# A transformer block on one core: a PSUM bank moved from products to scores, and the dilated heads' transposes issued behind the next group's scores

## The chip, the cores and the metric

The kernel runs on one core of a Trainium2 chip. The metric is the device time of one execution in microseconds. Three runs of the kernel before took 2779.58, 2775.93 and 2775.42 us; their median is 2775.93 us. A fourth execution was profiled, and all rows below are from it.

## The reference

One block on a sequence of 2048 tokens of width 1024, float32. A conditioning vector gives scales, shifts and gates for two normalisations. The normalised input goes through one product with a 1024 x 2816 matrix (IN_WIDTH), whose columns feed three mixers; their outputs are put together, multiplied with `w_out`, gated and added to x. A feed-forward part with a causal convolution of width 3 and a final normalisation follow. The mixers, cut:

```
def _spatial_gating(u, v, g_sgu, w_sp, b_sp):          # "a": 4 groups of 64
    u, v = gelu(u), rmsnorm(gelu(v).reshape(..., 4, 64))
    mixed = einsum('gts,bnsgc->bntgc', tril(w_sp), v) + b_sp
    return u * mixed

def _stick_breaking(q, k, v):                          # 6 heads of 64
    z = einsum('bqhd,bkhd->bhqk', q_blk, k) * scale
    log_beta = log_sigmoid(z)
    log_stay = where(before, log_sigmoid(-z), 0.0)
    tail = cumsum(log_stay, axis=3, reverse=True) - log_stay
    weight = where(before, exp(log_beta + tail), 0.0)
    return einsum('bhqk,bkhd->bqhd', weight, v)

def _dilated_window(q, k, v):                          # 6 heads of 64, dilations 1, 1, 4, 4, 16, 16
    idx = q_pos - offsets * dil                        # 129 offsets: every dil-th key back
    z = einsum('bqhd,bqmhd->bqhm', q_blk, k[idx]) * scale
    z = where(idx >= 0, z, -inf)
    p = exp(z - max(z)); denom = sum(p)
    o = einsum('bqhm,bqmhd->bqhd', p, v[idx]) / denom
    return o, max(z) + log(denom)                      # then weighed over the three dilations
```

## The kernel before, in words

The sequence is worked in 2 chunks of 1024 tokens, each in 2 groups of 512. Every product is made of three matmuls: both factors are split into a high and a low part (fp32r), and high x high, high x low and low x high are added in PSUM. Operands that come from PSUM are therefore stored twice: a copy gives the high part, a subtraction on VectorE (DVE) the low part.

The input product is cut into units of weight columns. `unit_t` (matmuls at L100 to L102, tile `gm`, 24 matmuls of 512 columns) makes transposed queries and keys; `unit_v` (L342, tile `gmv`, 48 matmuls of 256 columns) makes values. Each product fills one PSUM bank and is copied out of it in halves by ScalarE (ACT), DVE or both: `stage<-gm` for queries and keys, `vst<-gmv` for values. The weights are loaded by DMA as `wraw` and split into `whi` (mostly on ACT, L70) and `wlo`.

`stick(h, c)` works one stick-breaking head. Per block of 128 queries and 512 keys: scores into a bank (tile `z`, L534 to L537), two sigmoids on ACT (L539, L540, the second writes back into the bank), a scan along the keys on DVE (`excl<-z`, L545), a product on GpSimd (`beta`), transposes into a bank (tile `tr`, L554), high and low copies (`wh`, `wl`), and the matmuls with the values (tile `av`, L565). The bank of the scores is free once the scan has read it.

`dilated(h)` works one head of the dilated mixer in a loop over 8 groups of 256 queries (two blocks of 128). Per group: scores of both blocks in one bank (`zc`, L620 and L621), mask and maximum on DVE (`ec<-zc`, L623, tile `stat`), its negative (`mx`, L625), the exponential with its sum on ACT (L632), transposes into a bank (`trc`, L635), high and low copies (`whc`, `wlc`), and matmuls with the values (`avc`, L658). Two groups share one `avc` bank, which is then folded and stored.

PSUM has 8 banks. From the start to the marker `rel` (0 to some 785 us) one pool, `ps`, serves all of this: 3 banks for products (tag gm), 2 for scores of both mixers (z), 2 for transposes (tr) and 1 for weighted values (av). Behind `rel` a new pool, `ps2`, has 2 for products and 3 for scores. The first group's products (L910) are made in banks given by name, 4 for queries and keys (`("gm", "gm", "gm", "z")`) and 2 for values.

The string `ORDER` says in which order units of the product and heads are traced, with units interleaved between the steps of heads. Within it, a scheduler with a simulated timeline (`TileContext(schedule_with_timeline_sim=True)`) sets the order of the instructions of each engine; `tc.issue_after(x)` adds an edge that keeps what is traced under it behind instruction x. On the chip each engine then works its instructions strictly in that order.

Of the kernel before, what the change touches and what calls it, by code (L numbers as in the profile page):

```python
# [5 lines left out]
F32 = mybir.dt.float32  # L6
# [3 lines left out]
AF = mybir.ActivationFunctionType  # L10
# [5 lines left out]
P = 128  # L16
# [27 lines left out]
class Kernel:  # L44
# [529 lines left out]
    def dilated(self, h):  # L574
        nc = self.nc
        pair, row = h // 2, (h % 2) * 64
        d = DIL[pair]
        u, col = (6 + h) // 4, ((6 + h) % 4) * P
        vd = self.vd[u]

        def vloads(gg):
            def f(v):
                if d == 1:
                    return [(v, vd[gg][:, col:col + P].rearrange("(b p) f -> p b f", p=P))]
                if d == 4:
                    return [(v[:, 4 * r + 2 * cc:4 * r + 2 * cc + 2, :],
                             vd[cc].rearrange("(b p r) f -> r p b f", r=4, p=P)[2 * gg + r, :, :, col:col + P])
                            for r in range(2) for cc in range(2)]
                return [(v[64 * cc:64 * cc + 64],
                         vd[cc].rearrange("(p r) f -> p r f", r=16)[:, 8 * gg:8 * gg + 8, col:col + P])  # L590
                        for cc in range(2)]
            return f

        khat, vhat = [], []
        for gg in range(2):
            khat.append(self.head_keys(self.ck[pair][h % 2, :, :, gg * T:(gg + 1) * T]))
            vhat.append(self.head_values(vloads(gg)))
        stat = self.pa.tile([P, 16, 2], F32, name="stat", tag="stat")
        mx = self.pa.tile([P, 16], F32, name="mx", tag="mx")
        per = 16 // d  # L600
        for g in range(8):
            if g % 2 == 0:
                q1, q2 = self.head_queries(self.cq[pair][h % 2, :, :, g * 256:g * 256 + 512])
            qo = (g % 2) * 256
            z = self.ps.tile([P, 2, 256], F32, name="zc", tag="z")
            e = self.pa.tile([P, 2, 256], F32, name="ec", tag="beta")
            for j in range(2):
                blk = 2 * g + j
                first = blk % per == 0
                qs = slice(qo + j * P, qo + (j + 1) * P)  # L610
                qa, qb = q1[:, qs], q2[:, qs]
                own = khat[blk // 8][:, (blk % 8) * P:(blk % 8 + 1) * P]
                if first:
                    spans = [(slice(P, 2 * P), own)]
                elif blk % 8 == 0:
                    spans = [(slice(0, P), khat[blk // 8 - 1][:, 7 * P:8 * P]), (slice(P, 2 * P), own)]
                else:
                    spans = [(slice(0, 2 * P), khat[blk // 8][:, (blk % 8 - 1) * P:(blk % 8 + 1) * P])]
                for sl, kk in spans:
                    nc.tensor.matmul(z[:, j, sl], qa, kk, start=True, stop=False)  # L620
                    nc.tensor.matmul(z[:, j, sl], qb, kk, start=False, stop=True)  # L621
                ks = slice(P, 2 * P) if first else slice(0, 2 * P)
                nc.vector.tensor_tensor_reduce(e[:, j, ks], z[:, j, ks], self.mask[:, ks], 0.125, -3.0e38,  # L623
                                               ALU.add, ALU.max, stat[:, blk, 0:1])
            nc.vector.tensor_scalar(out=mx[:, 2 * g:2 * g + 2], in0=stat[:, 2 * g:2 * g + 2, 0], scalar1=-1.0,  # L625
                                    scalar2=None, op0=ALU.mult)
            tr = self.ps.tile([P, 4, P], F32, name="trc", tag="tr")
            for j in range(2):
                blk = 2 * g + j
                first = blk % per == 0  # L630
                ks = slice(P, 2 * P) if first else slice(0, 2 * P)
                nc.scalar.activation(e[:, j, ks], e[:, j, ks], AF.Exp, bias=mx[:, blk:blk + 1],  # L632
                                     accum_out=stat[:, blk, 1:2])
                for m in ((1,) if first else (0, 1)):
                    nc.tensor.transpose(tr[:, 2 * j + m, :], e[:, j, m * P:(m + 1) * P], self.ident)  # L635
            wh = self.pa.tile([P, 4, P], F32R, name="whc", tag="wh")
            wl = self.pa.tile([P, 4, P], F32R, name="wlc", tag="wl")
            if (2 * g) % per and (2 * g + 1) % per:
                parts = [slice(0, 4)]
            elif (2 * g) % per == 0 and (2 * g + 1) % per == 0:  # L640
                parts = [slice(1, 4, 2)]
            else:
                parts = [slice(1, 4)]
            for sl in parts:
                self.copy("whi_d", wh[:, sl, :], tr[:, sl, :])
                self.tt("v", wl[:, sl, :], tr[:, sl, :], wh[:, sl, :].bitcast(F32), ALU.subtract)
            if g % 2 == 0:
                av2 = self.ps.tile([P, 512], F32, name="avc", tag="av")
            av = av2[:, qo:qo + 256]
            kb = 2 * g  # L650
            if per == 1:
                sets = [[(kb + j, j, 1, 2 * j + 1)] for j in range(2)]
            else:
                sets = [[(kb, 0, 2, 1), (kb + 1, 1, 1, 3)] + ([(kb - 1, 0, 1, 0)] if kb % per else [])]
            for ops in sets:
                for n, (k, j, m, o) in enumerate(ops):
                    for x, w in enumerate((wh, wl)):
                        nc.tensor.matmul(av[:, j * P:(j + m) * P], vhat[k // 8][:, k % 8, :], w[:, o:o + m, :],  # L658
                                         start=(n == 0 and x == 0), stop=(n == len(ops) - 1 and x == 1))
            if g % 2 == 1:  # L660
                ys = self.pa.tile([64, 512], F32, name="ys", tag="ys")
                self.fold(ys, av2, 512)
                self.load(self.yc[pair][row:row + 64, (g // 2) * 512:(g // 2 + 1) * 512], ys)
        sd = self.statd[h]
        if d == 1:
            self.load(sd.rearrange("(b p) s -> p b s", p=P), stat)
        elif d == 4:
            for r in range(4):
                self.load(sd.rearrange("(b p r) s -> r p b s", r=4, p=P)[r], stat[:, 4 * r:4 * r + 4, :])
        else:  # L670
            self.load(sd.rearrange("(p r) s -> p r s", r=16), stat)
# [183 lines left out]
    def run(self):  # L855
# [44 lines left out]
        def qk_cols(p):  # L900
# [6 lines left out]
        near = (self.p1, "whi"), (self.p1, "wlo")  # L907
        places = ((near, near), (near, ((self.pa, "khat"), (self.pa, "khat"))),
                  (((self.pa, "vhat"), (self.pa, "khat")), ((self.pa, "vhat"), (self.pa, "wl"))))
        banks = [self.ps.tile([P, TG], F32, name="gm", tag=tag) for tag in ("gm", "gm", "gm", "z")]  # L910
        vbanks = [self.ps.tile([P, 2, 256], F32, name="gmv", tag=tag) for tag in ("z", "av")]
        for q in range(4):
            self.ada_first(q)
# [133 lines left out]
        for c, order in enumerate(ORDER):  # L1047
            u = units(c, hT[c])
            for token in order.split():
# [38 lines left out]
                elif what == "rope":  # L1088
                    cs = self.rope_tables(c)
                elif what == "ada":  # L1090
                    with tc.issue_after(self.stored.ins):
                        ada[n] = self.ada_rest(n)
                elif what == "dil":
                    finish([f"cqk{n // 2}{c}", f"v{(6 + n) // 4}{c}"])
                    self.dilated(n)
                elif what == "scales":
                    self.dilated_scales()
                elif what == "rel":
                    finish()
                    self.p1.release()  # L1100
                    self.ps.release()
                    self.ps = _Bufs(self.pool("ps2", space=PSUM), {**BUFS, "gm": 2, "z": 3})
                    self.po = _Bufs(self.pool("po"), BUFS)
                elif what == "free":
                    finish()
                    self.pa.release()
                    self.pw = _Bufs(self.pool("pw", side="right"), BUFS)
                    self.pn = _Bufs(self.pool("pn", side="right"), BUFS)
# [43 lines left out]

ENGINES = {"whi0": "a", "wlo0": "v", "lnt0": "a", "hlo0": "v", "lnt": "va", "lnx00": "avv", "lnx01": "aav", "lnx10": "v", "lnx11": "v", "lnx": "va", "hlo": "v", "whi": "a", "wlo": "v", "qkhi": "avv", "qklo": "v", "cqk": "a", "rot1": "v", "rot2": "v", "rot3": "v", "rothi": "aav", "rotlo": "v", "sgu1": "v", "sgu2": "v", "sguhi": "a", "sgulo": "v", "ya": "aaav", "fold": "a", "beta": "p", "whi_s": "a", "whi_d": "avv", "wom": "v", "wohi": "aav", "wolo": "v", "ysc": "v", "yhi": "av", "ylo": "v", "wuhi": "v", "wulo": "pvv", "wdm": "p", "wdhi": "av", "wdlo": "ppv", "upc": "av", "gv": "pppv", "ghi": "ap", "glo": "ppv", "vhi": "av", "vlo": "v", "uc": "v"}

BUFS = {"gm": 3, "z": 2, "tr": 2, "av": 1, "wraw": 2, "whi": 3, "wlo": 3, "s8": 3, "cs": 2, "tmp2": 2, "khat": 3, "vhat": 2, "q": 2, "beta": 4, "excl": 3, "wh": 2, "wl": 2, "fold": 1, "ys": 1, "stat": 2, "mx": 2, "x4": 2, "yraw": 2, "ysc": 4, "yh": 2, "yl": 2, "xo": 3, "wuraw": 4, "wul": 3, "wuh": 3, "wdraw": 2, "fx": 2, "up": 3, "dn": 5, "wdh": 2, "wdl": 2, "upc": 3, "cv": 3, "gh": 4, "gl": 4, "fs": 4, "fry": 2, "frr": 2}

WOUT = 6
EARLY = (0, 1, 5, 6, 7)
# [39 lines left out]
```

## Time and profile before

| | us |
|---|---|
| median of three runs | 2775.93 |
| the profiled execution | 2772.08 |
| its span, first to last instruction | 2770.4 |
| TensorE matmul busy | 2626.6 (95%) |
| VectorE busy | 2109.4 (76%) |
| ScalarE busy | 1025.6 (37%) |
| GpSimd busy | 857.5 (31%) |

The mean granted clock of TensorE was 0.981 of full speed. "Busy" counts the time in which at least one instruction of that engine was executing; matmuls overlap, so that one of 0.39 us can start every 0.23 us. A row of the timeline gives start, duration, engine, line and operands, and in brackets how long the engine stood idle before and what ended it. A name in a row is that of the tile in the code: `z` and `zc` are scores, `tr` and `trc` transposes, `gm` and `gmv` products.

### The profile page before, as it was taken

The page shows a single profiled execution, that of the slowest core. Times are in us where ns is not written, and L with a number is a line of the kernel's source. Part 1 is how long each engine was busy: PE and PEld are TensorE (multiplying, and loading weights), DVE is VectorE, ACT ScalarE, POOL GpSimd, SP SyncE. Part 2 cuts the span into 40 slices and gives each one's busy share as a digit, 9 for nine tenths or more (in the row PEclk, how much of TensorE's full clock was granted, in tenths as well). Part 3 has the DMA queues.
Part 4 walks back from the last instruction along what each step waited for, and adds up shares of the span by engine and source line. Part 5 has one row for each costly group of instructions (what it writes and reads, how often), then busy time and mean ns, then how long its engine had stood idle before and what let it go on. Part 6 is the DMA issues. An engine that isn't in the chain of part 4 may idle for free.

```text
span 2770.4 us, 36801 instructions
## 1 busy us (share of the span) xinstructions
PE 2626.6 (95%) x13430; PEld 2201.3 (79%) x13430; DVE 2109.4 (76%) x3227; ACT 1025.6 (37%) x1918; POOL 857.5 (31%) x878
## 2 busy tenths in 40 slices
PE   6989999899878999999999999999999999999998
PEld 5878998889857777877788888888877888888886
DVE  5487877666689988756877778777888778777877
ACT  5355554444556666534121212111462111121114
POOL 0032101110045444303334443433433433433423
PEclk9999999999999999999999999999999999999999
DMA  7645586789563333286111111111233111111111
GB/s 238 195 131 171 186 266 190 204 211 233 135 186 101 109 111 86 61 275 219 46 46 46 54 51 49 48 52 46 77 103 107 49 47 54 46 46 46 46 38 61
DMA packets 305296, 309.37 MB, mean 112 GB/s; under 512 B 65516, under 2 KB 245596, under 8 KB 305116
## 3 DMA queue, kind: packets, MB, share of 16 engines
q1 hardware_dynamic: 305116, 307.02, 37.6%
q8 instruction: 107, 1.75, 0.3%
q14 instruction: 73, 0.60, 0.1%
HBM read 232.36 MB, written 68.30 MB: 109 GB/s over the span
## 4 chain that ended last, share of the span: by engine, by line
PE 65%; DVE 14%; DMA 10%; ACT 6%; issue 3%; SPq 1%; POOL 0%; DVEq 0%; ACTq 0%; POOLq 0%
PE up L94 11%; PE up L93 11%; PE up L92 11%; PE dn L94 5%; PE dn L92 5%; PE dn L93 5%; DVE excl L545 3%; DMA wraw<-in_w_in_dram 2%; PE gmv L342 2%; DMA wada<-in_w_ada_dram 2%; PE av L565 2%; DVE wl L78 1%; PE gm L100 1%; PE tr L554 1%; PE gm L101 1%
## 5 line engine op out<-in xcount | busy, mean ns | idle before, releaser
L92 PE MATMUL up<-gh,wuh 128*128 128x512 f32 x1408 | 553.4, 393 | 2.1 <-ACT gh L260 2.1
L94 PE MATMUL up<-gh,wul 128*128 128x512 f32 x1408 | 554.9, 394 | 0.0
L93 PE MATMUL up<-gl,wuh 128*128 128x512 f32 x1408 | 554.5, 394 | 0.0
L78 POOL TENSOR_TENSOR beta<-beta,excl 128x127 f32<-128x127 f32 (+2 forms) x240 | 267.5, 1116 | 869.6 <-DVE excl L545 758.5
L829 DVE TENSOR_TENSOR acc<-dn,acc 128x512 f32<-128x512 f32 x688 | 440.7, 680 | 104.2 <-PE dn L94 102.0
L787 DVE SCALAR_TENSOR_TENSOR cv<-upc,cw,cv 128x512 f32<-128x512 f32 x352 | 334.8, 952 | 104.9 <-ACT cv L785 101.6
L92 PEld LDWEIGHTS up<-gh,wuh 128*128 128x128 f32 x1408 | 265.0, 188 | 62.1 <-ACT gh L260 2.3
L93 PEld LDWEIGHTS up<-gl,wuh 128*128 128x128 f32 x1408 | 265.1, 188 | 61.3 <-issue 0.2
L94 PEld LDWEIGHTS up<-gh,wul 128*128 128x128 f32 x1408 | 265.1, 188 | 60.0 <-issue 0.2
L92 PE MATMUL dn<-wdh,gh 128*128 128x512 f32 x688 | 270.9, 395 | 10.6 <-DVE acc L829 9.4
L93 PE MATMUL dn<-wdl,gh 128*128 128x512 f32 x688 | 270.9, 394 | 0.0
L94 PE MATMUL dn<-wdh,gl 128*128 128x512 f32 x688 | 256.1, 395 | 0.0
L785 ACT ACTIVATE cv<-up,cb 128x512 f32<-128x512 f32 x176 | 136.4, 775 | 290.9 <-DVE upc L72 290.9
L545 DVE TENSOR_TENSOR_SCAN excl<-z,excl,beta 128x512 f32<-128x512 f32 x144 | 183.3, 1275 | 14.9 <-ACT z L540 13.2
L70 ACT ACTIVATE upc<-up 128x512 f32<-128x512 f32 x88 | 52.4, 596 | 373.8 <-PE up L94 373.8
L70 ACT ACTIVATE wh<-tr 128x128 fp32r<-128x128 f32 (+2 forms) x240 | 127.7, 535 | 168.4 <-PE tr L554 164.8
L72 DVE CAST wuh<-wuraw 128x512 fp32r<-128x512 f32 x176 | 129.0, 771 | 62.0 <-PE up L93 59.7
L342 PE MATMUL gmv<-whi,hh 128*128 128x256 f32 x576 | 167.0, 291 | 0.7 <-DVE vst L78 0.7
L342 PE MATMUL gmv<-wlo,hh 128*128 128x256 f32 x576 | 166.6, 290 | 0.3 <-DVE wlo L78 0.3
L342 PE MATMUL gmv<-whi,hl 128*128 128x256 f32 x576 | 166.7, 291 | 0.0
L78 DVE TENSOR_TENSOR wl<-tr,wh 128x128 fp32r<-128x128 f32 (+2 forms) x240 | 141.9, 594 | 31.6 <-ACT wh L70 31.6
L92 PEld LDWEIGHTS dn<-wdh,gh 128*128 128x128 f32 x688 | 129.8, 189 | 42.6 <-DVE acc L829 11.6
(238 smaller groups left out, 5594.8 us busy)
## 6 DMA issues: line engine op xcount, KB each, us to landing
wuraw<-in_w_up_dram SPq DMA_DIRECT2D x176, 256.0 KB, 3.2
wdraw<-in_w_down_dram SPq DMA_DIRECT2D x44, 512.0 KB, 3.5
wada<-in_w_ada_dram SPq DMA_DIRECT2D x32, 512.0 KB, 6.2
wraw<-in_w_in_dram SPq DMA_DIRECT2D x112, 128.0 KB, 4.3
vd<-vst SPq DMA_DIRECT2D x12, 1024.0 KB, 6.0
q<-bq SPq DMA_DIRECT2D x48, 256.0 KB, 4.2
q<-cq SPq DMA_DIRECT2D x48, 256.0 KB, 5.5
x<-xo SPq DMA_DIRECT2D x24, 512.0 KB, 5.2
```

What stands on the lines that cost most here:

```text
L70: self.nc.scalar.activation(out, in_, AF.Copy)
L72: self.nc.vector.tensor_copy(out, in_)
L78: (self.nc.vector if eng == "v" else self.nc.gpsimd).tensor_tensor(out=out, in0=a, in1=b, op=op)
L92: self.nc.tensor.matmul(ps, ah, bh, start=(k == 0), stop=False)
L93: self.nc.tensor.matmul(ps, ah, bl, start=False, stop=False)
L94: self.nc.tensor.matmul(ps, al, bh, start=False, stop=(k == n - 1))
L342: self.nc.tensor.matmul(ps[:, e, :], a[:, o:o + P], b, start=(n == 0), stop=(n == 3 * KB - 1))
L545: nc.vector.tensor_tensor_scan(x[:, x0:x0 + n][:, ::-1], z[:, :n][:, ::-1], b[:, :n][:, ::-1], before, op0=ALU.mult, op1=ALU.bypass)
L565: last = nc.tensor.matmul(av[:, q0:256], vhat[kc // 2][:, (kc % 2) * 4 + e, :], w[:, e, q0:256], start=(kc == top and m == 0), stop=(kc == ...
L785: nc.scalar.activation(t, ps, AF.Identity, bias=self.cb[:, blk:blk + 1], scale=self.cw[2][:, blk:blk + 1])
L787: nc.vector.scalar_tensor_tensor(out=t, in0=u[:, tap:tap + TG], scalar=self.cw[tap][:, blk:blk + 1], in1=t, op0=ALU.mult, op1=ALU.add)
L829: nc.vector.tensor_tensor(out=acc[t][:, ns], in0=ps, in1=acc[t][:, ns], op=ALU.add)
```

## The change

The body of the loop in `dilated` becomes two inner functions. `scores(g)` has the scores, the maximum, its negative and the exponentials; it returns the tile of exponentials and the last score matmul. `weights(g, e)` has the transposes and the high and low copies. The loop traces `scores(g + 1)` first, and `weights(g, e)` behind it under `issue_after` of the last score matmul of group g + 1. The pool's table BUFS gives 2 banks to products and 3 to scores (3 and 2 before); of the first group's banks, one more has the tag z; the pool behind `rel` takes BUFS as it is, which has the same numbers as it had. The instructions of every engine are the same in kind and number, but for ACT, which has 4 table loads fewer.

```diff
         per = 16 // d
-        for g in range(8):
+        def scores(g):
             if g % 2 == 0:
-                q1, q2 = self.head_queries(self.cq[pair][h % 2, :, :, g * 256:g * 256 + 512])
+                q12[:] = self.head_queries(self.cq[pair][h % 2, :, :, g * 256:g * 256 + 512])
+            q1, q2 = q12
...
                     nc.tensor.matmul(z[:, j, sl], qa, kk, start=True, stop=False)
-                    nc.tensor.matmul(z[:, j, sl], qb, kk, start=False, stop=True)
+                    mm = nc.tensor.matmul(z[:, j, sl], qb, kk, start=False, stop=True)
...
             nc.vector.tensor_scalar(out=mx[:, 2 * g:2 * g + 2], in0=stat[:, 2 * g:2 * g + 2, 0], scalar1=-1.0,
                                     scalar2=None, op0=ALU.mult)
+            for j in range(2):
+                blk = 2 * g + j
+                ks = slice(P, 2 * P) if blk % per == 0 else slice(0, 2 * P)
+                nc.scalar.activation(e[:, j, ks], e[:, j, ks], AF.Exp, bias=mx[:, blk:blk + 1],
+                                     accum_out=stat[:, blk, 1:2])
+            return e, mm.ins
+
+        def weights(g, e):
             tr = self.ps.tile([P, 4, P], F32, name="trc", tag="tr")
             for j in range(2):
-                blk = 2 * g + j
-                first = blk % per == 0
-                ks = slice(P, 2 * P) if first else slice(0, 2 * P)
-                nc.scalar.activation(e[:, j, ks], e[:, j, ks], AF.Exp, bias=mx[:, blk:blk + 1],
-                                     accum_out=stat[:, blk, 1:2])
-                for m in ((1,) if first else (0, 1)):
+                for m in ((1,) if (2 * g + j) % per == 0 else (0, 1)):
                     nc.tensor.transpose(tr[:, 2 * j + m, :], e[:, j, m * P:(m + 1) * P], self.ident)
...
+            return wh, wl
+
+        q12 = [None, None]
+        ahead = scores(0)
+        for g in range(8):
+            e = ahead[0]
+            if g + 1 < 8:
+                ahead = scores(g + 1)
+                with self.tc.issue_after(ahead[1]):
+                    wh, wl = weights(g, e)
+            else:
+                wh, wl = weights(g, e)
+            qo = (g % 2) * 256
             if g % 2 == 0:
                 av2 = self.ps.tile([P, 512], F32, name="avc", tag="av")
...
-        banks = [self.ps.tile([P, TG], F32, name="gm", tag=tag) for tag in ("gm", "gm", "gm", "z")]
+        banks = [self.ps.tile([P, TG], F32, name="gm", tag=tag) for tag in ("gm", "gm", "z", "z")]
...
-                    self.ps = _Bufs(self.pool("ps2", space=PSUM), {**BUFS, "gm": 2, "z": 3})
+                    self.ps = _Bufs(self.pool("ps2", space=PSUM), BUFS)
...
-BUFS = {"gm": 3, "z": 2, "tr": 2, "av": 1,
+BUFS = {"gm": 2, "z": 3, "tr": 2, "av": 1,
```

Lines of the changed kernel are its own (transposes L641, dilated scores L622 and L623, their matmuls with the values L678). The orders of the two kernels are the same up to some 83 us of the trace of before and again from some 860 us. Three places in between follow; the number behind a tile's name tells one tile of that name from another.

The first is on ACT, at the start of a dilated head (exponentials `ec_7046` and on), where before copies of weights (`whi_8207`) and a Gelu (`u_7827`) stand. Before:

```order
L70 ACTIVATE whc_7012<-trc_7005 128x512
L70 ACTIVATE whi_8207<-wraw_8209 128x512
L425 ACT_TABLE_LOAD
L425 ACTIVATE u_7827<-u_7827 128x1024
L632 ACT_TABLE_LOAD
L632 ACTIVATE ec_7046,stat_7040<-ec_7046,mx_7041 128x128 x2
L632 ACTIVATE ec_7069,stat_7040<-ec_7069,mx_7041 128x128 x2
L70 ACTIVATE whi_8207<-wraw_8214 128x512
```

And now, from the last of that head's exponentials on:

```order
L632 ACTIVATE ec_7189,stat_7040<-ec_7189,mx_7041 128x128 x2
L632 ACTIVATE ec_7216,stat_7040<-ec_7216,mx_7041 128x128 x2
L70 ACTIVATE whc_7202<-trc_7199 128x2x128
L70 ACTIVATE fold_7158<-avc_7127 64x512
L70 ACTIVATE whi_7889<-wraw_7891 128x512
L70 ACTIVATE whi_7889<-wraw_7895 128x512
L705 ACTIVATE stats_7393<-stats_7393 128x96
L70 ACTIVATE fold_7211<-avc_7180 64x512
L425 ACT_TABLE_LOAD
L425 ACTIVATE u_7827<-u_7827 128x1024
L70 ACTIVATE whi_8207<-wraw_8209 128x512
L70 ACTIVATE whi_8207<-wraw_8214 128x512
```

The copies of `whi_8207` and the Gelu of `u_7827`, which stood ahead of the head's first exponentials (`ec_7046`), now stand behind its last ones (`ec_7216`).

The second is on TensorE, where the product `gm_2375` begins (at 141.19 us in the trace of before); `z`, `tr` and `av` there are of stick-breaking heads. Before:

```order
L100 MATMUL gm_2310<-hh_722,whi_2204 128x512
L101 MATMUL gm_2310<-hl_730,whi_2204 128x512
L102 MATMUL gm_2310<-hh_722,wlo_2205 128x512
L100 MATMUL gm_2375<-hh_231,whi_2350 128x512
L101 MATMUL gm_2375<-hl_239,whi_2350 128x512
L102 MATMUL gm_2375<-hh_231,wlo_2351 128x512
```

And now, the rows ahead of `gm_2375`:

```order
L565 MATMUL av_1211<-wh_1247,vhat_1119 128x256 x2
L534 MATMUL z_1415<-khat_1391,q_1395 128x256
L536 MATMUL z_1415<-after_678,ident_r_676 128x128
L537 MATMUL z_1415<-khat_1391,q_1395 128x256
L565 MATMUL av_1211<-wl_1248,vhat_1119 128x256
L565 MATMUL av_1211<-wh_1247,vhat_1119 128x256
L565 MATMUL av_1211<-wl_1248,vhat_1119 128x256
L565 MATMUL av_1211<-wh_1247,vhat_1119 128x256
L565 MATMUL av_1211<-wl_1248,vhat_1119 128x256 x2
L554 MATMUL tr_1315<-ident_60,beta_1309 128x128 x4
L100 MATMUL gm_2375<-hh_231,whi_2350 128x512
```

Between the last matmul of `gm_2310` and the first of `gm_2375` there was nothing before; now 42 rows stand there, with six tiles of scores (`z_1289` to `z_1415`), their transposes and the matmuls with the values.

The third is on TensorE, where the values product `gmv_5375` begins (at 495.64 us before), beside the first dilated head (`zc`, `trc`, `avc`) and a stick-breaking head (`z_5493`, `z_5507`). Before:

```order
L342 MATMUL gmv_5321<-wlo_5258,hh_3831 128x256
L342 MATMUL gmv_5321<-whi_5257,hl_3839 128x256
L342 MATMUL gmv_5375<-whi_5247,hh_4046 128x256
L342 MATMUL gmv_5375<-wlo_5248,hh_4046 128x256
L635 MATMUL trc_4915<-ident_60,ec_4907 128x128 x2
L342 MATMUL gmv_5375<-whi_5247,hl_4054 128x256
```

And now, from the fourth of five matmuls of `avc_4937` on, which follow the last one of `gmv_5321`:

```order
L678 MATMUL avc_4937<-whc_4965,vhat_4836 128x128
L678 MATMUL avc_4937<-wlc_4966,vhat_4836 128x128
L534 MATMUL z_5493<-khat_5483,q_5487 128x128
L536 MATMUL z_5493<-after_678,ident_r_676 128x128
L537 MATMUL z_5493<-khat_5483,q_5487 128x128
L641 MATMUL trc_4991<-ident_60,ec_4948 128x128 x4
L641 MATMUL trc_5021<-ident_60,ec_4981 128x128 x2
L622 MATMUL zc_5041<-khat_4838,q_5007 128x256
L623 MATMUL zc_5041<-khat_4838,q_5007 128x256
L641 MATMUL trc_5021<-ident_60,ec_4981 128x128 x2
L534 MATMUL z_5507<-khat_5483,q_5487 128x256
L342 MATMUL gmv_5375<-whi_5247,hh_4046 128x256
```

The two products followed each other directly, with transposes (`trc_4915`) two matmuls into the second; now matmuls with values, the scores of a stick-breaking head and the transposes of two groups stand between them, and the transposes of `ec_4948` stand behind scores of later groups.

## Rows read from the trace of the kernel before

**Rows 1.** The page: busy time of the engines; loads of queries.
```profile
PE 2626.6 (95%) x13430; PEld 2201.3 (79%) x13430; DVE 2109.4 (76%) x3227; ACT 1025.6 (37%) x1918; POOL 857.5 (31%) x878
...
q<-cq SPq DMA_DIRECT2D x48, 256.0 KB, 5.5
```

**Rows 2.** Windows: length, busy by engine (PE, PEld, DVE, ACT, POOL), clock, DMA.
```profile
75.00:785.00 710.00, 663.34 (x4346) 598.45 (x4347) 500.77 (x956) 342.36 (x725) 94.34 (x81) 0.98 0.69 192
```

**Rows 3.** Waits of PE, 75 to 785 us: us in total, times, longest.
```profile
PE z L534 <- DVE excl L545: 17.2, 14, 4.5
PE trc L635 <- ACT ec L632: 14.1, 8, 7.5
...
PE zc L620 <- DVE stat L623: 3.0, 3, 1.3
...
PE gmv L342 <- DVE vst L78: 0.7, 2, 0.4
```

**Rows 4.** Windows of four stretches at clock 0.50, columns as in rows 2.
```profile
157.10:163.90 6.80, 5.85 (x15) 4.65 (x16) 6.80 (x7) 4.49 (x9) 4.24 (x3) 0.50 0.48 110
242.50:245.90 3.40, 3.05 (x13) 3.05 (x14) 3.40 (x6) 0.87 (x2) 2.15 (x2) 0.50 0.00 0
...
536.00:539.40 3.40, 3.40 (x11) 2.66 (x10) 2.08 (x5) 1.36 (x5) 1.83 (x3) 0.50 0.91 263
713.50:723.70 10.20, 4.76 (x23) 4.77 (x24) 3.94 (x15) 7.31 (x15) 0.00 (x0) 0.50 0.84 181
```

**Rows 5.** Timeline of PE, where four long idle times end.
```profile
158.05 0.80 PE L534 MATMUL z<-khat,q 128*128 128x512 f32 x1 [3.62 <-DVE excl L545]
...
242.85 0.69 PE L534 MATMUL z<-khat,q 128*128 128x384 f32 x1 [3.13 <-DVE excl L545]
...
535.38 0.33 PE L534 MATMUL z<-khat,q 128*128 128x128 f32 x1 [4.53 <-DVE excl L545]
...
718.94 0.48 PE L635 MATMUL trc<-ident,ec 128*128 128x128 f32 x1 [7.48 <-ACT ec L632]
```

**Rows 6.** Timelines of DVE and ACT ahead of two of these.
```profile
156.77 1.22 DVE L545 TENSOR_TENSOR_SCAN excl<-z,beta 128x512 f32<-128x512 f32 x1 [1.07 <-issue]
...
532.23 1.35 ACT L70 ACTIVATE whi<-wraw 128x512 fp32r<-128x512 f32 x2 [7.05 <-DMA wraw<-in_w_in_dram]
```

**Rows 7.** Timeline of ACT ahead of the transpose at 718.94.
```profile
714.08 0.63 ACT L70 ACTIVATE whi<-wraw 128x512 fp32r<-128x512 f32 x1 [8.13 <-DMA wraw<-in_w_in_dram]
714.73 1.28 ACT L425 ACT_TABLE_LOAD   x1
```

**Rows 8.** Timeline of PE at four products that use a third bank.
```profile
141.19 0.39 PE L100 MATMUL gm<-hh,whi 128*128 128x512 f32 x1
141.42 0.39 PE L101 MATMUL gm<-hl,whi 128*128 128x512 f32 x1
...
317.84 0.28 PE L342 MATMUL gmv<-whi,hh 128*128 128x256 f32 x1
...
384.16 0.28 PE L342 MATMUL gmv<-whi,hh 128*128 128x256 f32 x1
...
495.64 0.28 PE L342 MATMUL gmv<-whi,hh 128*128 128x256 f32 x1
495.76 0.28 PE L342 MATMUL gmv<-wlo,hh 128*128 128x256 f32 x1
```

**Rows 9.** Timelines of ACT and DVE: copies of the products two before those.
```profile
158.55 1.10 ACT L70 ACTIVATE stage<-gm 128x512 f32<-128x512 f32 x2
...
323.31 0.41 DVE L78 TENSOR_TENSOR vst<-gmv,vst 128x256 fp32r<-128x256 f32 x1
...
390.18 0.41 DVE L78 TENSOR_TENSOR vst<-gmv,vst 128x256 fp32r<-128x256 f32 x1
...
504.73 0.64 ACT L70 ACTIVATE vst<-gmv 128x256 fp32r<-128x256 f32 x2
```

**Rows 10.** Waits of ACT, 75 to 785 us, columns as in rows 3.
```profile
ACT whi L70 <- DMA wraw<-in_w_in_dram: 84.3, 25, 8.2
```

More of the change, by code (lines that the diff above doesn't have):

```diff
@@ L1153 @@
 ENGINES = {"whi0": "a", "wlo0": "v", "lnt0": "a", "hlo0": "v", "lnt": "va", "lnx00": "avv", "lnx01": "aav", "lnx10": "v", "lnx11": "v", "lnx": "va", "hlo": "v", "whi": "a", "wlo": "v", "qkhi": "avv", "qklo": "v", "cqk": "a", "rot1": "v", "rot2": "v", "rot3": "v", "rothi": "aav", "rotlo": "v", "sgu1": "v", "sgu2": "v", "sguhi": "a", "sgulo": "v", "ya": "aaav", "fold": "a", "beta": "p", "whi_s": "a", "whi_d": "avv", "wom": "v", "wohi": "aav", "wolo": "v", "ysc": "v", "yhi": "av", "ylo": "v", "wuhi": "v", "wulo": "pvv", "wdm": "p", "wdhi": "av", "wdlo": "ppv", "upc": "av", "gv": "pppv", "ghi": "ap", "glo": "ppv", "vhi": "av", "vlo": "v", "uc": "v"}
-BUFS = {"gm": 3, "z": 2, "tr": 2, "av": 1, "wraw": 2, "whi": 3, "wlo": 3, "s8": 3, "cs": 2, "tmp2": 2, "khat": 3, "vhat": 2, "q": 2, "beta": 4, "excl": 3, "wh": 2, "wl": 2, "fold": 1, "ys": 1, "stat": 2, "mx": 2, "x4": 2, "yraw": 2, "ysc": 4, "yh": 2, "yl": 2, "xo": 3, "wuraw": 4, "wul": 3, "wuh": 3, "wdraw": 2, "fx": 2, "up": 3, "dn": 5, "wdh": 2, "wdl": 2, "upc": 3, "cv": 3, "gh": 4, "gl": 4, "fs": 4, "fry": 2, "frr": 2}
+BUFS = {"gm": 2, "z": 3, "tr": 2, "av": 1, "wraw": 2, "whi": 3, "wlo": 3, "s8": 3, "cs": 2, "tmp2": 2, "khat": 3, "vhat": 2, "q": 2, "beta": 4, "excl": 3, "wh": 2, "wl": 2, "fold": 1, "ys": 1, "stat": 2, "mx": 2, "x4": 2, "yraw": 2, "ysc": 4, "yh": 2, "yl": 2, "xo": 3, "wuraw": 4, "wul": 3, "wuh": 3, "wdraw": 2, "fx": 2, "up": 3, "dn": 5, "wdh": 2, "wdl": 2, "upc": 3, "cv": 3, "gh": 4, "gl": 4, "fs": 4, "fry": 2, "frr": 2}
 WOUT = 6
```

## The prediction

> **What bounds the kernel now.** I began with the busy times. TensorE (PE) is busy for 2626.6 of 2770.4 us; no other engine comes near it [rows 1]. So time can only be won where PE stands idle or runs at its slower clock, and lost where it is made to stand. I then cut the span to the stretch that the changed pool serves and in which most moved instructions lie, 75 to 785 us: PE busy 663.34 of 710.0 us, so 46.7 us idle; DVE busy 500.77, ACT 342.36 [rows 2]. DVE and ACT have room on average, so a PE wait there is a matter of order and buffers, not of capacity.
>
> Next I asked what PE waits for in that stretch [rows 3]. Stick-breaking scores wait for the scan that frees their PSUM bank: 17.2 us in 14 waits. Dilated transposes wait for the exponentials: 14.1 us in 8, of which one is 7.5. Dilated scores wait for the reduce on DVE (tile stat): 3.0 us. A product waits for its bank 0.7 us in two waits: with three banks, products are all but free of such waits.
>
> Last came the clock. Four stretches were granted 0.50 of TensorE's clock, 1.2 instead of 2.4 GHz, with 5.85, 3.05, 3.40 and 4.76 us of PE work in them [rows 4]. Each lies around or behind a long idle time of PE: 3.62, 3.13, 4.53 and 7.48 us [rows 5]. Work at half clock costs half its time, so they cost 2.9, 1.5, 1.7 and 2.4 us, and a removed stall would take this with it.
>
> **A. A third score bank.** It can remove at most the 17.2 us of waits and the half-clock work behind three of them, (5.85 + 3.05 + 3.40) / 2 = 6.2: 23.4 us. It can also remove nothing: at 158.05 PE waits for a scan that DVE starts only at 156.77, behind 1.07 us in which it waits for nothing that the profile shows [rows 6]. What makes that scan late is not the banks; a score that goes a bank earlier would be scanned no sooner, and the transposes would wait instead. The wait that ends at 535.38 has another reason: ACT takes up two copies of weights that wait for their load (7.05 us), and the sigmoids stand behind them [rows 6]. In the changed order the copies stand behind three pairs of sigmoids, so that this wait should go. With rows for both ends I take half: **-11.7** (0 to -23.4).
>
> **B. Scores one group ahead.** In the worst stall, PE's transpose at 718.94 waits 7.48 us for an exponential. ACT's rows say why: it waits 8.13 us for a load of weights, copies them, loads the Gelu table (1.28 us), and comes to the exponentials only behind the Gelu and a load of their own table [rows 7]. The changed ACT order has these exponentials, and those of the head's other groups, ahead of the copies (first order fence); one Gelu with its two table loads stays among them. I take the whole stall, 7.48 + 2.4 of clock = 9.9. What else the lookahead can hide is the other trc waits, 14.1 - 7.5 = 6.6, and 3.0 for the reduce: 9.6. The order before already had two groups' scores ahead of a head's first transposes, so that much of the cover existed: I take a third, 3.2. Sum **-13.1** (-6 if a shorter wait takes the place of the big one, -19.5 if all goes).
>
> Four ACT table loads fewer are 4 x 1.28 = 5.1 us of ACT time [rows 7]. ACT is busy 342.36 of 710.0 us [rows 2], so nothing beyond the stall above is credited. The loads of queries (tile q, 48 of 256 KB, 5.5 us to landing [rows 1]) are asked for one group earlier, as are their scores. The transposes now queue on PE behind scores that need them: where such a load is late, PE stands for up to 5.5 us and the transposes with it. The waits before name no load of queries, so I take 0 and keep one such wait, 5.5, in the range.
>
> **C. One product bank less.** This is the price. A product of 24 matmuls starts one every 0.23 us, so lasts 24 x 0.23 = 5.5 us; one of values has 48 matmuls at 0.12, 5.6 us by 0.117 unrounded [rows 8]. Before, PE makes use of the third bank where the copies come late. The product that starts at 141.19 goes ahead while the two before it are not copied out until 158.55. The values product at 495.64 does so while ACT comes to the one two back at 504.73. Two more values products start at 384.16 and 317.84, and the ones two back have copies that start as late as 390.18 and 323.31 [rows 8, 9]. I price these four. With two banks each of these must start later or have other work ahead of it. Upper end: nothing covers, 5.5 + 3 x 5.6 = 22.3 us, plus the half clock behind each. Lower end: the new order covers all, 0. The second and third order fences show what it puts there: at the first place score, transpose and weighted-value matmuls of two query groups stand between the products; at the second some transposes and scores. But these wait themselves for the sigmoids, scans and exponentials that keep ACT and DVE from the copies. I take two of the four places in full, one of each kind, 5.5 + 5.6 = 11.1, and for each a restart at half clock at the price of the short stretch, 3.05 / 2 = 1.5: **+14.1** (0 to +28.3).
>
> The rows of these four places show a third bank in use. The Trainium skill asks for no more than rotation (Perfetto Trace Analysis, section Matmuls, under Optimizing Tensor Performance): independent matmul groups "should rotate through different PSUM banks so the ACT/DVE evacuation of one overlaps the next group's matmuls". Two banks already rotate; by that rule C would be 0 and the sum -24.8. The trace of before agrees with it where the copy comes within one product's 5.5 us, and at the four places it does not.
>
> The first group's products and the later stages: the number of banks is the same there (gm and z exchange one; the later pool keeps its numbers), and the orders agree up to 83 us and from about 860 us. No term.
>
> **Sum.** -11.7 - 13.1 + 14.1 = -10.7 us on the profiled execution's own 2772.08: 2761.4. The median of the three runs, 2775.93, lies 3.85 above that execution, so the forecast is **2765** for the median. A difference of 0.2%, 5.55 us, is about what a measurement of this kernel can tell: faster means below 2770.4, slower above 2781.5.
>
> **Rivals.**
> *Product banks decide (slower).* DVE and ACT copy a product in the turn that the scheduler gave; with two banks PE stands at all four places, 22.3 us, with four restarts of 1.5: +28.3. The score banks then help little, because the wait only moves from z to gm (a quarter, -5.9), and of B only the one stall is sure (-9.9): +12.5, 2784.6 on its own, **2788** for the median. It decides as soon as C passes A + B = 24.8. For it: the late copies of rows 9. Against it: most of the span's products have copies within one product, and the order does put other work between.
> *Waits only move (no change).* ACT waits 84.3 us for loads of weights in this stretch [rows 10], in 25 waits, and the DMA engines are busy 0.69 of it [rows 2], 0.84 at the big stall [rows 4]. The copies, moved behind the exponentials, would then hold up the next product instead: the 9.9 comes back one product later. With A and C at half, -11.7 + 14.1, and -3.2, the sum is -0.8: **2775**. That the lookahead does not do what it says belongs here: the scheduler already put two groups of scores first.
> *Two banks are enough (faster by more).* The matmuls that the new order puts between products last until the copies are done, so that C = 0: 2772.08 - 24.8 = 2747.3, **2751** for the median. The rule of the Trainium skill named above points this way. The late copies of rows 9 speak against it: 158.55 is 17 us behind the third product's start.
>
> **How the numbers follow.** My forecast has a chance of 0.40 (0.36 of it faster, 0.04 within 0.2%), with a range of its own from 2756 to 2771; product banks decide 0.26 (all slower); waits only move 0.24 (0.21 the same, 0.02 slower, 0.01 faster); two banks are enough 0.10 (faster). That makes faster 0.47, same 0.25, slower 0.28. The range runs from 2752, which leaves out half of the last rival (0.05), to 2788, which leaves out half of the slower one (0.13); one late load of queries (5.5) on top of the likeliest case lies within it. The ends at which everything goes one way (-42.9, +22.3) need all bounds at once and are left out.
>
> **What would show it.** *A* is right if waits of z for the scan fall from 17.2 to some 8 and the half-clock stretches behind 158, 243 and 535 us get fewer. *B* is right if no transpose waits above 3 us for an exponential and the stall at 711 us is gone. *C* is right if new waits of gm or gmv for stage or vst appear, some 11 us in all between 75 and 785 us. PE's idle time there should fall from 46.7 to about 39, since some 3 us of the gain is clock. The stages behind 860 us should keep their lengths within a microsecond. The prediction is wrong if waits for product banks exceed 25 us (then slower), if they are near zero (then below 2755), or if the end of the stretch moves by less than 3 us while waits change their names.

## The result: slower by 1.35%, and the profile after

The changed kernel takes 2810.44 us (median of six runs, 2805.77 to 2821.93), the kernel before 2774.48 (six runs): a ratio of 1.0135, 95% interval 1.012 to 1.0151. I had forecast 2765 in a range that ended at 2788.

The profiled execution took 2808.42 us, its span is 2806.5, so 36.1 longer than that of before. The busy times of its page, beside [rows 1]:

```profile
PE 2636.0 (94%) x13430; PEld 2210.9 (79%) x13430; DVE 2121.6 (76%) x3227; ACT 1018.7 (36%) x1914; POOL 847.7 (30%) x878
```

The same matmuls, 9.4 us more of PE busy and the rest as idle time. The stretch that answers to [rows 2] is 74.2 to 820.6 us. I found its ends by counting the columns that had streamed through TensorE: at these times the two kernels had done the same amount. Columns as in rows 2:

```profile
74.20:820.60 746.40, 676.68 (x4345) 611.57 (x4346) 509.98 (x954) 335.34 (x720) 88.49 (x81) 0.96 0.66 183
```

The stretch is 36.4 us longer (746.4 against 710.0). Of this, 23.0 is idle time of PE (69.7 against 46.7) and 13.3 is PE busy for the same work (676.68 against 663.34), with the granted clock at 0.96 instead of 0.98. The waits of PE in it, beside [rows 3]:

```profile
PE zc L622 <- DMA q<-cq: 20.9, 11, 5.6
PE av L565 <- DVE wl L78: 6.5, 5, 2.1
PE z L534 <- DVE excl L545: 5.7, 11, 1.1
...
PE gm L102 <- DVE wlo L78: 3.4, 1, 3.4
...
PE gmv L327 <- DVE hl L78: 3.2, 3, 1.9
PE gmv L342 <- DVE vst L78: 2.9, 1, 2.9
...
PE gm L100 <- DVE vst L78: 1.6, 1, 1.6
```

By names, the change did what it set out to do: the wait of scores for the scan fell from 17.2 to 5.7 us, and the transposes' wait for exponentials, 14.1 before, is not in the list. Yet the kernel is slower. Products wait for a bank (a copy `vst` still to be read out) 2.9 + 1.6 = 4.5 us in all. The largest wait is new: dilated scores for their queries, 20.9 us.

Where the time goes shows when one follows the columns. The changed kernel is behind by 13.8 us where the one before stands at 160 us, by some 6 at 250, by 26.1 at 400, by 26.6 at 610 and by 35.6 at 785 (a count of columns swings by some us where work has changed places); behind 860 us nothing is added (36.2 near the end). So some 20 of the 36 us are lost between 250 and 400 us, where no dilated head runs. That stretch before:

```profile
250.00:400.00 150.00, 146.91 (x1111) 139.49 (x1109) 118.48 (x188) 80.17 (x139) 19.81 (x18) 1.00 0.69 226
```

and the same work now:

```profile
255.90:426.10 170.20, 153.12 (x1110) 145.00 (x1109) 121.72 (x193) 78.08 (x134) 15.23 (x16) 0.96 0.65 202
```

PE was idle for 3.1 us in it and always at full clock; now it is idle for 17.1 and part of the work runs at half clock. The waits there are many and small, and only the first in this list is at a product's bank:

```profile
PE gmv L342 <- DVE vst L78: 2.9, 1, 2.9
PE gmv L342 <- DVE wlo L78: 2.7, 2, 2.5
PE av L565 <- DVE wl L78: 2.0, 2, 1.8
PE ya_ps L454 <- DVE u L449: 1.9, 1, 1.9
PE mix_ps L443 <- ACT vs L70: 1.6, 1, 1.6
PE z L534 <- DVE excl L545: 1.6, 3, 1.1
PE ln_ps L257 <- DVE ln_tmp L262: 1.5, 1, 1.5
```

PE runs at the lower of its two clock levels, 1.2 instead of 2.4 GHz, in four stretches of 3.4 us there, where before it had none between 246 and 467 us. The first of them:

```profile
310.60:314.00 3.40, 3.40 (x20) 3.40 (x17) 3.40 (x4) 2.58 (x4) 1.09 (x1) 0.51 0.03 7
```

It lies behind this wait in PE's timeline:

```profile
307.32 0.28 PE L342 MATMUL gmv<-whi,hl 128*128 128x256 f32 x1
307.44 0.28 PE L342 MATMUL gmv<-whi,hh 128*128 128x256 f32 x1
309.52 0.39 PE L565 MATMUL av<-wl,vhat 128*128 128x256 f32 x1 [1.80 <-DVE wl L78]
...
311.76 0.41 PE L342 MATMUL gmv<-whi,hl 128*128 128x256 f32 x1
311.97 0.41 PE L342 MATMUL gmv<-whi,hh 128*128 128x256 f32 x1
```

The weighted values (`av`) stand in the middle of a product and wait for a subtraction on DVE (tile `wl`), which had work of the gating mixer first:

```profile
307.64 1.23 DVE L433 TENSOR_TENSOR v<-v,rs_r 128x1024 f32<-128x1024 f32 x1
308.78 0.68 DVE L78 TENSOR_TENSOR wl<-tr,wh 128x512 fp32r<-128x512 f32 x1
```

Behind the 1.80 us the product goes on at one matmul in 0.21 us where it had been 0.12. So this wait was paid for twice, as idle time and as work at half clock.

### The profile page after: what moved, and what is told of

Same layout as the page of the kernel before. It is cut to its first block, busy times and chain, and to the rows that moved or that the text cites. A ratio compares the mean times of both kernels' runs of the same rounds, so it can differ in the third digit from the quotient of the medians.

```text
span 2806.5 us, 36803 instructions
## 1 busy us (share of the span) xinstructions
PE 2636.0 (94%) x13430; PEld 2210.9 (79%) x13430; DVE 2121.6 (76%) x3227; ACT 1018.7 (36%) x1914; POOL 847.7 (30%) x878
## 4 chain that ended last, share of the span: by engine, by line
PE 67%; DVE 13%; DMA 11%; ACT 4%; issue 3%; SPq 1%; POOL 0%; DVEq 0%; ACTq 0%
PE up L92 11%; PE up L94 11%; PE up L93 11%; PE dn L94 5%; PE dn L92 5%; PE dn L93 5%; PE gmv L342 4%; DVE excl L545 3%; PE av L565 2%; DMA q<-cq 2%; DMA wada<-in_w_ada_dram 2%; DVE wl L78 1%; SPq L83 1%; PE gm L100 1%; PE gm L101 1%
## 5 line engine op out<-in xcount | busy, mean ns | idle before, releaser
L78 POOL TENSOR_TENSOR beta<-beta,excl 128x127 f32<-128x127 f32 (+2 forms) x240 | 259.8, 1086 | 907.5 <-DVE excl L545 703.9
L92 PE MATMUL dn<-wdh,gh 128*128 128x512 f32 x688 | 270.9, 395 | 10.9 <-DVE acc L849 9.6
```

The lines of the kernel that those rows point to most:

```text
L78: (self.nc.vector if eng == "v" else self.nc.gpsimd).tensor_tensor(out=out, in0=a, in1=b, op=op)
L92: self.nc.tensor.matmul(ps, ah, bh, start=(k == 0), stop=False)
```

## The experiments

Theory 1: the lost product bank costs the time, since products are what TensorE does while other work is waited for. Theory 2: the loss comes from scores put ahead of transposes, which then stand behind loads of queries. Theory 3: both, independently. Ratios are against the kernel before, run on the same chip beside each. The first four runs take the change apart.

**The banks alone.** The loop of dilated heads is the old one, and the pool behind `rel` keeps its numbers.

```diff
-        banks = [... for tag in ("gm", "gm", "gm", "z")]
+        banks = [... for tag in ("gm", "gm", "z", "z")]
-BUFS = {"gm": 3, "z": 2, "tr": 2, "av": 1, ...}
+BUFS = {"gm": 2, "z": 3, "tr": 2, "av": 1, ...}
```

> The banks of the change alone (2 for products, 3 for scores), with the loop of dilated heads as before. Theory 1, the third product bank is what was lost: TensorE's order is that of the changed kernel until the dilated heads are well under way, and the changed kernel is some 26 us behind by the start of its first dilated head (469.1 before, 493.1 in it, for the first dilated scores), so at least 24 us of the 36 come here: 2796 to 2806 us where before takes 2774. Theory 2, the loss comes from scores put ahead of transposes, which then wait for loads of queries: this kernel has none of that and is near before or a little faster, 2765 to 2780 us, since it keeps the third score bank. Theory 3, both and independent: about +25 here and +10 in the kernel with the lookahead alone.

Measured: 2805.56 against 2772.11 us, ratio 1.0112 (1.0085 to 1.014). This fits theory 1: 33 of the 36 us, by the medians, come with the banks (by the ratios 31 of 37). Theory 2 falls too: the wait for queries is there without the lookahead.

```profile
PE zc L620 <- DMA q<-cq: 13.2, 9, 3.6
```

**The lookahead alone**: the changed loop with its edge, and the banks of before (the banks' part of the diff undone).

> The lookahead alone (scores of the next group and the edge behind them), with 3 product and 2 score banks as before. Theory 1, product banks: same as before until the first dilated head, and within 6 us of it at the end, 2768 to 2780 us. Theory 2, transposes behind scores that wait for query loads: most of the 36 us, 2795 us and more, with over 15 us of dilated scores waiting for loads of q. Theory 3, both: +8 to +15 us, 2782 to 2790, with the stall of the transposes at 711 us replaced by waits for q.

Measured: 2775.41 against 2772.11 us, ratio 1.0018 (0.9997 to 1.004): nothing that can be told from no change. Theory 3, by which some 10 us of the loss would be the lookahead's, falls too. The first 400 us are as before (less than 1 us apart in columns). Its profiled execution, 2782.28 us, was a longer one than the median. Its waits of PE, 75 to 795 us:

```profile
PE z L534 <- DVE excl L545: 12.3, 12, 3.6
PE zc L622 <- DVE stat L625: 10.9, 5, 7.6
PE trc L641 <- ACT ec L632: 6.9, 5, 2.9
```

The transposes' wait fell from 14.1 to 6.9 us, and the scores' wait for the reduce rose from 3.0 to 10.9. The stall at 711 us is still there, under another name. Where it ends in PE's timeline:

```profile
726.47 0.47 PE L622 MATMUL zc<-khat,q 128*128 128x128 f32 x1 [7.65 <-DVE stat L625]
```

What ACT did ahead of it:

```profile
724.85 0.63 ACT L70 ACTIVATE whi<-wraw 128x512 fp32r<-128x512 f32 x1 [10.90 <-DMA wraw<-in_w_in_dram]
```

And DVE:

```profile
725.51 0.69 DVE L78 TENSOR_TENSOR wlo<-wraw,whi 128x512 fp32r<-128x512 f32 x1 [10.41 <-ACT whi L70]
726.12 0.28 DVE L625 CUSTOM_DVE_ANT_0 ec<-zc,mask 128x128 f32<-128x128 f32 x1
```

ACT waits for the load of weights as in [rows 7]. Before, exponentials stood behind that copy on ACT. Here the low half `wlo` waits for the copy on DVE, and the reduce that frees the scores' bank stands behind it.

**Without the edge**, with the new banks and with the old ones:

```diff
-                with self.tc.issue_after(ahead[1]):
-                    wh, wl = weights(g, e)
+                wh, wl = weights(g, e)
```

> The changed kernel without the edge: scores of the next group are traced first, but the scheduler may put the transposes ahead of them. Theory 1: the loss of the first 470 us stays, the dilated stretch is as in the changed kernel or a few us better: 2800 to 2812 us. Theory 2: waits of dilated scores for loads of q fall from 20.9 us to under 8, and most of the 36 us goes: 2780 us or less. Theory 3: the wait for q goes and the banks' loss stays: 2796 to 2804 us.

Measured: 2806.41 us, ratio 1.0116 (1.0085 to 1.0147). The wait for queries is 12.7 us (20.9 with the edge): the edge makes at most a part of it.

> The lookahead in trace order alone, without the edge and with the banks of before (3 for products, 2 for scores). Theory 1: like before, 2768 to 2780 us. Theory 2: like before too, since the edge is gone, 2768 to 2780, and clearly faster than the lookahead with its edge. Theory 3: between, 2770 to 2782.

Measured: 2776.93 us, ratio 1.0017 (1.0 to 1.0034), as with the edge.

**Is it the product bank that went, or the score bank that came?** Two banks for each; the eighth (x) takes one tile of the first group and lies idle.

```diff
-        banks = [... for tag in ("gm", "gm", "gm", "z")]
+        banks = [... for tag in ("gm", "gm", "x", "z")]
-BUFS = {"gm": 3, "z": 2, ...}
+BUFS = {"gm": 2, "z": 2, ...}
```

> As before, but 2 banks for products and still 2 for scores; the eighth bank serves only the first group's products and lies idle from some 120 us on. It prices the loss of the product bank without the gain of a score bank. If the product bank decides and the third score bank is worth the 11.7 us I forecast for it, this is 10 to 15 us slower than the kernel with the new banks alone (2805 us): 2815 to 2820. If the third score bank is worth nothing here, the same as that kernel, 2800 to 2810. If instead the score bank is what does harm (it lets scores run ahead and bunch the dilated heads), this is near before, 2770 to 2785.

Measured: 2806.91 us, ratio 1.0123 (1.0107 to 1.0139). The loss is the product bank's: 33.7 us by the medians (2806.91 against 2773.21). The score bank made no difference: 2805.56 us and a ratio of 1.0112 with it. Its waits of PE, 75 to 814.5 us, show that the shorter wait for the scan isn't its work either:

```profile
PE trc L635 <- ACT ec L632: 11.4, 5, 7.2
PE z L534 <- DVE excl L545: 6.7, 10, 1.5
```

With two score banks as before, the wait for the scan is 6.7 us, not 17.2.

**The bank given back to a part.** The idle bank goes to every third product, of tile `gmv` in one kernel (values, and the inputs of the gating mixer, which share the name), of queries and keys in the other.

```diff
+    def bank(self):
+        n = self.turn["bank"] = self.turn.get("bank", -1) + 1
+        return ("gm", "gm", "x")[n % 3]
...
-            ps = self.ps.tile([P, 2, 256], F32, name="gmv", tag="gm")
+            ps = self.ps.tile([P, 2, 256], F32, name="gmv", tag=self.bank())
```

> The kernel with 2 product and 2 score banks (2806.9 us), with its idle eighth bank given to every third product of the kind gmv (values and the gating mixer's u and v). Nothing else has a third bank. If the bank counts wherever products follow each other closely, most of the 33 us comes back, since values make up most of the products from 280 to 430 us, where 20 us were lost, and beside the dilated heads: 2775 to 2790 us. If what counts is that products of both kinds share three banks, little comes back: 2798 to 2810.

> The same, with the eighth bank given to every third product of the kind gm (transposed queries and keys) instead. By the place of the loss I expect the smaller part here, mostly the 8 to 14 us between 75 and 160 us: 2792 to 2802 us. If the place does not matter, as much as in the run for values.

Measured: 2793.16 us for values (ratio 1.0079, 1.0051 to 1.0108), 2782.3 for queries and keys (1.0038, 1.0024 to 1.0052). Both bring time back. I had expected more from values; by the medians queries and keys bring more, though the two intervals just touch. The work of 250 to 400 us takes 170.0 us with the bank idle:

```profile
259.30:429.30 170.00, 152.32 (x1113) 143.72 (x1113) 119.07 (x192) 79.18 (x136) 20.55 (x18) 0.97 0.64 200
```

162.4 us with the bank for values (in an execution of 2779.91 us, the shortest of the six):

```profile
255.80:418.20 162.40, 151.91 (x1114) 142.32 (x1113) 121.50 (x194) 79.08 (x136) 21.18 (x18) 0.97 0.66 214
```

and 154.4 with the bank for queries and keys, at full clock again:

```profile
253.30:407.70 154.40, 147.13 (x1115) 139.75 (x1114) 122.14 (x193) 82.16 (x141) 21.12 (x19) 1.00 0.70 227
```

In this last kernel that stretch holds 96 matmuls of queries and keys, four products, beside 740 of `gmv`, some fifteen. At most two of the nineteen products there can be in the third bank, and yet most of the loss is gone. That points to the order that the scheduler makes rather than to products that stand at a full bank, but no run separates the two.

**Is it the time until a bank is read out?** Products that are read out twice, by a copy and a subtraction (stick-breaking queries and keys, and values), here have the low half computed from the high half in SBUF, so that the copy alone frees the bank. The low part is then zero, that is, both kernels leave it out.

```diff
-        self.tt(elo, lo, src, hi.bitcast(F32), ALU.subtract)
+        self.tt(elo, lo, hi.bitcast(F32) if ehi in ("qkhi", "vhi") else src, hi.bitcast(F32), ALU.subtract)
```

> The kernel before, with the low half of transposed queries and keys and of values computed from the high half in SBUF (its low part left out: the subtraction gives zeros), so that a product's bank is free after the copies and not after the subtractions. With three product banks TensorE hardly waits for them, so I expect the time of before within 5 us, 2767 to 2777 us, under every theory.

> The new banks alone (2 for products, 3 for scores, loop as before), with the same early release of product banks (the low half left out). If the loss is the time that a full product bank waits for both of its readers, an earlier release gives part of the 33 us back: 2780 to 2797 us. If the copies themselves come late (the bank waits for its turn on ACT and DVE, whichever is second), little comes back: 2800 to 2808. If the loss is only in the order that the scheduler makes, and not in bank time, none comes back either, but then its waits also stay where they are.

Measured: 2770.87 us with the old banks (ratio 0.9991, 0.9966 to 1.0015), 2802.91 with the new ones (1.0104, 1.0085 to 1.0123). The 32 us between the two stay. That the second reader holds the bank is not the cause. Whether the first reader is too late, or the scheduler's order alone loses the time, these runs don't tell.

**Is it only the setting of the interleaving?** New banks, other rates of products between steps.

```diff
-RATE = (0.354, 3.21)
+RATE = (0.3, 2.7)
```

> The new banks alone (2805 us), with fewer products put between the steps of stick-breaking heads (the pair RATE at 0.30, 2.7 in place of 0.354, 3.21). Theory 1, a bank too few: the time hardly changes, 2798 to 2815 us. Rival, the rate was set for three banks and only has to be set anew for two: one of this run and the next comes down by more than 15 us, to 2790 or less.

> The new banks alone, with more products between the steps (0.41, 3.7). Theory 1: 2798 to 2820 us, rather slower, since more products come closer together than two banks take. Rival, the rate only has to be set anew: 2790 or less in this run or the one before.

Measured: 2818.99 (1.0174, 1.0143 to 1.0204) and 2806.2 us (1.0127, 1.0093 to 1.0161). The rival falls as far as two rates can show it: neither comes near the kernel before. The first lies above the 2815 us that I gave as its upper end.

**Other uses of eight banks.** Four for products and one for transposes, first.

> As before, but 4 banks for products, 2 for scores and 1 for transposes in the first pool. If TensorE lacks filler because products fill their banks, a fourth one gives a little more than the third where transposes allow it: 2765 to 2775 us, and waits of transposes of 10 us and more appear, which may eat it (2775 to 2795). If the bank count of products has no such effect beyond the third, only the loss by the transposes' bank shows: 2780 us and more.

Measured: 2919.25 us, ratio 1.0537 (1.0513 to 1.056). The second bank of transposes is worth far more than I expected. The run with three for products, two for scores, one for transposes and an idle one is the base of the next:

> As before (3 for products, 2 for scores), but 1 bank for transposes in the first pool; the eighth bank is not used. It is the base for the next run. Transposes of one block must wait until the block before is copied: with four product banks and this one transpose bank the kernel took 2919 us, so I expect 2860 to 2930 us here.

> The same with the eighth bank given to scores: 3 for products, 3 for scores, 1 for transposes. If the third score bank takes away waits that end at the score bank, as my prediction had it, 10 us or more below the run with 2 score banks. If the scores wait for the scan whichever bank they are in, and the wait only changes its name, the same within 8 us.

Measured: 2913.29 us (1.0514, 1.0491 to 1.0537) and, with the third score bank, 2933.47 (1.0575, 1.0545 to 1.0605). A fourth product bank gave nothing beside these 2913.29, and the third score bank cost 20 us. The waits of scores, 75 to 930 us, in the kernel with two score banks:

```profile
PE z L534 <- DVE excl L545: 11.5, 13, 2.3
...
PE zc L620 <- DMA q<-cq: 4.6, 1, 4.6
```

and with three:

```profile
PE zc L620 <- DMA q<-cq: 22.5, 10, 4.8
...
PE z L534 <- DVE excl L545: 11.4, 12, 2.2
```

The wait for the scan is the same with either; the wait for queries grows by 17.9 us. It goes with the third score bank in the other kernels, too: 13.2 and 12.7 us with the banks alone and without the edge, 20.9 in the changed kernel, and 2.2 with two score banks and an idle one. My reading is that a third bank lets scores be ordered further ahead than the two buffers of queries reach. A third buffer of queries would test this; no run has one. No version that I ran beats the kernel before by more than noise.

**Could any change of the order have cost this?** An edit can make the scheduler put out another order, and a single pair of kernels could differ by chance of that order. The runs together speak against it. With two banks for transposes throughout, the four kernels that have three product banks took 2771 to 2777 us, and the seven that have two took 2803 to 2819.

## Why the prediction was wrong, step by step

*What bounds the kernel* held: the whole loss is idle time and half clock of PE within the stretch of [rows 2], and the stages behind 860 us kept their lengths.

*A, -11.7 for the third score bank*, failed. The wait it was to remove did get shorter in name, 17.2 to 5.7 us, but it is 6.7 with two score banks as well. In both pairs that differ in this bank alone nothing came back (2806.91 and 2805.56; 2913.29 and 2933.47). I took a wait that ends at a full bank for a lack of banks. The lower end that I gave, nothing, was right, and I had the reason at hand: the scan itself was late [rows 6].

*B, -13.1 for the lookahead*, failed: the run of it alone gives +3, within noise of zero. I took the stall at 711 us as sure. In the trace of the lookahead alone the same chain begins at a load of weights: ACT waits 10.90 us for it, and now the reduce on DVE stands behind it, where the exponentials on ACT stood before. The "waits only move" rival said this, with another place.

*The query loads, taken at 0*, were mis-sized: 20.9 us of waits. I looked for the risk in the edge, but neither the edge nor the lookahead is needed for them. In the kernel with the idle bank they are 2.2 us and the time is the same, so that they are no term of their own in the sum either.

*C, +14.1 for the product bank*, is the step that decides, and was right in sign and too small: 33.7 us by the run that takes away this bank alone. My upper end was 28.3. I priced it at the four places where the trace shows three banks full at once, by the length of one product. At the first of them the loss came: by columns the changed kernel goes from 6.6 us behind at 140 us of before to 13.8 at 160. But PE hardly stands at a product's bank (4.5 us for `vst`), and more is lost where I had priced only two products, between 250 and 400 us. The signs that I gave were wrong as well: 4.5 us of such waits, far from 25, would have meant at most a small loss, and the falling waits of A and B a gain. They looked at the names of waits, while PE's idle time rose to 69.7 us instead of falling to 39. My reading of the traces is that products are the work that the order puts under the waits of everything else; with a bank less they come elsewhere, and waits of 1 to 3 us are bare that were covered before, with work at half clock behind them. This is argued from the traces and not shown by a run. Shown is that the bank costs the time and where; how much of it the scheduler's order makes, and how much the bank itself, stays open, since no run had the one without the other. With what the runs measured in place of my terms (A about 0, B +3, C +34) the sum is some +37, beside the 36 measured. No wait in the profile of before stands for such a loss, because there it is all cover. The warning was in rows that the prediction did not use: 3.1 us of idle time in 150, in a stretch full of products.

*The rivals.* "Product banks decide" had the right sign and the right bank, and 12.5 us where 36 came. Against "two banks are enough": the rule that groups of matmuls should rotate through banks so that one's evacuation lies under the next (the Trainium skill, Perfetto Trace Analysis, section Matmuls) was followed with two banks as with three. Here the number of banks mattered: 2807 us with two, 2782 and 2793 with a third for some products, 2774 with three for all.

## What to carry to other kernels

A buffer whose own waits are near zero may be what keeps an engine fed: before taking it away, look at how little idle time there is in the stages that it serves, and price the loss by what its work covers, not by its own waits. A wait that ends at a buffer shows who came last, not that a buffer is missing; ask whether that work would have started earlier. And where one late transfer holds a chain, moving one of the instructions behind it can just move the wait to another engine, as here from ACT's exponentials to DVE's reduce (7.48 and 7.65 us).

## What the runs showed of the hardware that I had not expected

A wait as short as 1.80 us was followed by work at half clock: matmuls 0.21 us apart instead of 0.12. In the trace of before I had seen it only beside the long stalls of [rows 5], and had counted it only with these. In the changed kernel 13.3 of 36 us are PE busy for the same work. In the stretch that was 250 to 400 us the longest wait is 2.9 us, and still its granted clock fell from 1.00 to 0.96.
